# Moving SBUF tiles to other starts modulo 128 bytes in a kernel of 32-bit matmuls on one NeuronCore

## Chip, cores and metric

One core of a Trainium2 chip runs one launch of the kernel. The metric is the device time of the launch in microseconds (us). The kernel before was timed three times: 2841.1 us is the median, 2837.99 and 2863.9 us are the ends.

## What is computed

256 tokens of width 2048 go through two transformer-like blocks. Nearly all the arithmetic is in matrix products of the tokens with float32 weight matrices, about 480 MB of weights in all:

```
# first block
proj   = rms_norm(x) @ w_in                       # 2048 x 11280
y_a    = gated_delta_rule(...) @ w_branch_a       # 8 heads, chunks of 64
y_b    = block_attention(...)  @ w_branch_b       # 8 heads
x      = x + (sigmoid(gate_a) * y_a + sigmoid(gate_b) * y_b) @ w_out
u      = causal_conv(rms_norm(x) @ w_up)          # 2048 x 11264
x      = x + (silu(u_gate) * u_val) @ w_down      # 5632 x 2048
x      = rms_norm(x)
# second block
z      = rms_norm(x) @ w_in_2                     # pooling branch and rwkv7 scan
x      = x + concat(pool_out, rwkv_out) @ w_out_2
x      = x + square(relu(rms_norm(x) @ w_ffn_up)) @ w_ffn_down   # 2048 x 8192 x 2048
x      = x + sigmoid(rms_norm(x) @ w_ple_gate) * (p @ w_ple_proj)
out    = rms_norm(x)
```

## The kernel before

Every large product is made from two float32r parts of each operand, a rounded value (hi) and what is left (lo): hi times hi, hi times lo and lo times hi are added up in PSUM. The weights come in pieces of 512 KB. `load_w` issues the DMA of a piece on SyncE's queue into `raw`, ScalarE copies it to `hi` (line 319) and VectorE subtracts to get `lo` (line 320); each of the three has three buffers. The activations' parts are made once for each product and stay in SBUF: `xhl` holds both parts of the normalized tokens, `hid`, `mh`, `ml`, `oah`, `obh` and others hold those of later stages.

Two helpers issue nearly all matmuls of TensorE.

- `wide_steps` makes outputs with features on the partitions. The weights are the stationary operand, 128 x 128 at a time, and the activations `xhl` stream past: 512 columns for the hi part of the weights (both parts of x, line 373) and 256 columns for their lo part (line 375). These two make a pair.
- `group_steps` makes outputs with tokens on the partitions. The activations are the stationary operand and the weights stream past, 512 columns at a time (256 in two short groups near the end): x hi with weights hi (line 345), x lo with weights hi (346), x hi with weights lo (347).

Each matmul instruction has its own load of the stationary operand (LDWEIGHTS, engine PEld in the profile), which runs beside the matmul ahead of it. In the stages with many small steps (the delta rule from about 200 to 500 us, the rwkv scan from about 1500 to 2000 us) a written-out order puts a few of these matmuls between the steps of a chain of other work.

Pools stack their tiles one behind the other along each partition, each tile at the next multiple of 32 bytes. The first constant table has 129 float32 columns (516 bytes), the small tiles (`tiny`, `rcol`, `hp` and so on) have 8 to 108 bytes, and all large tiles are multiples of 1024 bytes. So a few odd sizes decide where the large tiles start. In the built program they start at these places modulo 128 bytes:

| tile | before |
|---|---|
| `xhl` | 32 |
| `hi`, `lo` (all buffers) | 32 |
| `hid` of the second block; `oah`, `oal`, `mh`, most `ml` | 96 |
| `hid` of the first block: 8 of 11 groups, `obh`, `obl` | 0 |
| `hid` of the first block: 3 of 11 groups | 96 |
| `dhl0`; `dhl1` (pooling) | 96; 32 |

The pieces that one matmul reads of them lie at multiples of 512 bytes from there, except in the two narrow column groups (16 and 32 weight columns).

Of the kernel before, what the change touches and what calls it, by code (L numbers as in the profile page):

```python
# [10 lines left out]
F32 = mybir.dt.float32  # L11
# [8 lines left out]
KT = 16  # L20
KC = 2
NEG = -1e30
WINDOWS = (2, 4, 8, 16)


def _const_tables():
# [5 lines left out]
    def add(tables, name, a):  # L32
        for t in tables:
            t.append((name, np.broadcast_to(a, (128, a.shape[1])).astype(np.float32)))
# [4 lines left out]
    add([t1], "upper", (p <= f))  # L39
    add([t1], "gbias", np.where(p <= f, 0.0, NEG))  # L40
    add([t1], "amask", np.where(f <= p, 0.0, NEG))
    p64, f64 = p % 64, f[:, :64]
# [9 lines left out]
    add([t2], "rst", (np.arange(T)[None, :] % 64 != 0))  # L52
    for w in WINDOWS:
        add([t2], f"pc{w}", 1.0 / np.minimum(np.arange(16)[None, :] + 1, w))
# [67 lines left out]
def two_blocks_kernel(ctx: ExitStack, tc: tile.TileContext, I: dict, out: bass.AP):  # L122
    nc = tc.nc
# [3 lines left out]
    whi = ctx.enter_context(tc.tile_pool(name="whi", bufs=3))  # L127
    wlo = ctx.enter_context(tc.tile_pool(name="wlo", bufs=3))
    tmp = ctx.enter_context(tc.tile_pool(name="tmp", bufs=2))
# [11 lines left out]

    def load_consts(i, pool, queue):
        a, cols = CONSTS[i]
        t = pool.tile([128, a.shape[1]], F32, tag=f"C{i}", name=f"C{i}", bufs=1)
        queue.dma_start(t, I[f"consts{i}"])
        for name, (o, w) in cols.items():
            tabs[name] = t[:, o:o + w]

# [3 lines left out]
    def c(name, lo=0, hi=128):  # L152
        return tabs[name][lo:hi]

    load_consts(0, cpool, nc.sync)
    ident, one = c("ident"), c("one")

# [2 lines left out]
        return PT[t][lo:hi, o + i:o + i + n]  # L160

    cnt = [0]

    def nm(s):
        cnt[0] += 1
        return f"{s}_{cnt[0]}"
# [6 lines left out]
        return quad.tile(list(shape), dt, tag=f"Q{i}", name=nm(name))  # L173

    def tm(tag, F, dt=F32, bufs=2, p=128, pool=None):
        shape = [p] + (list(F) if isinstance(F, (tuple, list)) else [F])
        return (pool or tmp).tile(shape, dt, tag=tag, name=nm(tag), bufs=bufs)

    def wk(tag, F, dt=F32, bufs=2, p=128):
        return tm(tag, F, dt, bufs, p, quad)  # L180

    def psum(F=512, p=128):
        shape = [p] + (list(F) if isinstance(F, (tuple, list)) else [F])
        return ps.tile(shape, F32, tag="ps", name=nm("ps"))
# [26 lines left out]
    def other_params():  # L211
# [7 lines left out]
        for t in range(2):  # L219
            for i in range(NPT[t]):  # L220
                place_params(t, i, min(128, NROW[t] - 128 * i))

    ln_rows = tm("cva", T, bufs=3)[:16, :128]
    nc.scalar.dma_start(ln_rows, I["ln1"].rearrange("o (a b) -> (o a) b", b=128))

# [6 lines left out]
    def rsqrt(dst, src, t):  # L232

        ts(out=t.bitcast(I32), in0=src.bitcast(I32), scalar1=1, scalar2=None, op0=ALU.logical_shift_right)
        ts(out=dst.bitcast(I32), in0=t.bitcast(I32), scalar1=-1, scalar2=0x5F3759DF, op0=ALU.mult, op1=ALU.add)
        for f in (3.0, 12.0, 768.0):
            tt(out=t, in0=dst, in1=dst, op=ALU.mult)
            tt(out=t, in0=t, in1=src, op=ALU.mult)
            stt(dst, t, -f, dst, ALU.add, ALU.mult)
        ts(out=dst, in0=dst, scalar1=-1.0 / 8192, scalar2=None, op0=ALU.mult)  # L240

    def tiny(shape):
        return tm("tiny", shape, bufs=8)
# [145 lines left out]
    def wide(*a, **kw):  # L389
        for _ in wide_steps(*a, **kw):  # L390
            pass
# [117 lines left out]
    def gdn_gates():  # L509
        ab = tm("cva", T, bufs=3)[:16]  # L510
        wide(w_in, 3072, 16, xs, None, lambda m, p: act(ab, p, AF.Copy))
        hp = tm("hp", (2, 8), bufs=1)
        nc.gpsimd.dma_start(hp[:, 0], I["gdn_a_log"][0:1, :].to_broadcast([128, 8]))
        nc.gpsimd.dma_start(hp[:, 1], I["gdn_dt_bias"][0:1, :].to_broadcast([128, 8]))
        abt = tm("abt", (2, 16), bufs=1)
        p = psum()
        for i in range(2):
            nc.tensor.transpose(p[:, i * 16:(i + 1) * 16], ab[:, i * 128:(i + 1) * 128], ident[:16, :16])
        for i in range(2):
            ts(out=abt[:, i], in0=p[:, i * 16:(i + 1) * 16], scalar1=r1[:, i:i + 1], scalar2=None, op0=ALU.mult)  # L520

        act(t0, abt[:, :, 0:8], AF.Exp, scale=-1.0)
        ts(out=t0, in0=t0, scalar1=1.0, scalar2=None, op0=ALU.add)
        nc.vector.reciprocal(beta, t0)

        y = tm("y8", (2, 8), bufs=1)
        tt(out=y, in0=abt[:, :, 8:16], in1=hp[:, 1:2].to_broadcast([128, 2, 8]), op=ALU.add)
        ts(out=t0, in0=y, scalar1=0.0, scalar2=None, op0=ALU.max)
        stt(t1, t0, -2.0, y, ALU.mult, ALU.add)
        act(t1, t1, AF.Exp)  # L530
        sa = tm("sa8", (2, 8), bufs=1)
        s2 = tm("s28", (2, 8), bufs=1)
        ts(out=s2, in0=t1, scalar1=2.0, scalar2=None, op0=ALU.add)
        nc.vector.reciprocal(s2, s2)
        tt(out=sa, in0=t1, in1=s2, op=ALU.mult)
        tt(out=s2, in0=sa, in1=sa, op=ALU.mult)
        ts(out=t1, in0=s2, scalar1=2.0 / 17, scalar2=2.0 / 15, op0=ALU.mult, op1=ALU.add)
        for d in (13, 11, 9, 7, 5, 3, 1):
            tt(out=t1, in0=t1, in1=s2, op=ALU.mult)
            ts(out=t1, in0=t1, scalar1=2.0 / d, scalar2=None, op0=ALU.add)  # L540
        tt(out=t1, in0=t1, in1=sa, op=ALU.mult)
        tt(out=t0, in0=t0, in1=t1, op=ALU.add)
        ea = tm("ea8", 8, bufs=1)
        act(ea, hp[:, 0], AF.Exp)
        for i in range(2):
            stt(g[:, i], t0[:, i], -1.0, ea, ALU.mult, ALU.mult)
        p = psum()
        mm(p[:, 0:16], c("upper"), g, start=True, stop=True)
        mm(p[:, 16:32], c("ones"), g, start=False, stop=True, skip_group_check=True)
        nc.vector.tensor_copy(gc, p[:, 0:16].rearrange("p (a b) -> p a b", a=2))  # L550
        act(eg, gc, AF.Exp)
        tt(out=kds, in0=p[:, 16:32].rearrange("p (a b) -> p a b", a=2), in1=gc, op=ALU.subtract)
        act(kds, kds, AF.Exp)
        stt(nbe, beta, -1.0, eg, ALU.mult, ALU.mult)

    def gdn_scales(half):

        p = psum()
        for m in range(4):
            sq = wk("E", (2, 2, 128), bufs=1)  # L560
            act(sq, kq[half][m // 2][:, m % 2], AF.Square)
            for i in range(2):
                for j in range(2):
                    o = 8 * j + 4 * i + m
                    mm(p[:, o:o + 1], sq[:, i, j], one, start=(m == i == j == 0), stop=True, skip_group_check=True)
        hs = slice(4 * half, 4 * half + 4)
        n = tiny((2, 2, 4))
        ts(out=n, in0=p[:, :16].rearrange("p (a b c) -> p a b c", a=2, b=2), scalar1=1e-6, scalar2=None, op0=ALU.add)
        F = tm("gsc", (6, 2, 4))
        rsqrt(F[:, 0:2], n, tiny((2, 2, 4)))  # L570
        rk, rq, bk, kdr, nber, egq = (F[:, i] for i in range(6))
        ts(out=rq, in0=rq, scalar1=128 ** -0.5, scalar2=None, op0=ALU.mult)
        tt(out=bk, in0=beta[:, :, hs], in1=rk, op=ALU.mult)
        tt(out=kdr, in0=kds[:, :, hs], in1=rk, op=ALU.mult)
        tt(out=nber, in0=nbe[:, :, hs], in1=rk, op=ALU.mult)
        tt(out=egq, in0=eg[:, :, hs], in1=rq, op=ALU.mult)
        return rk, rq, bk, kdr, nber, egq
# [89 lines left out]
    def gdn_half(half):  # L667
        sc = gdn_scales(half)
        yield 12
        pre = []  # L670
        for m in range(4):
            pre.append(gdn_pre(4 * half + m, sc))
            yield 5
        Z = inverse16([p[0][:, 0] for p in pre], 2)
        yield 55
        for _ in rounds(gdn_inverse(pre[m:m + 2], Z[:, m:m + 2]) for m in (0, 2)):
            yield 6
        for m in (0, 2):
            for _ in rounds(gdn_post(4 * half + m + i, sc, pre[m + i]) for i in range(2)):
                yield 5  # L680
# [154 lines left out]
    for _ in gdn_proj(0):  # L835
        pass
    load_consts(1, quad, nc.sync)
    gdn_gates()
    other_params()

# [6 lines left out]
    for j, shift in ((0, 0.25), (1, 0.0)):  # L847

        n = tm("cva", T, bufs=3)[:32]
# [162 lines left out]
    oka = tm("oka", 8, bufs=1)  # L1012
# [16 lines left out]

    wide(w_in2, 4096, 288, xs, lambda: r4, ev_lora)  # L1030
    load_consts(2, quad, nc.sync)
    LW, GW, GV = ([wk(t, (4, 128), bufs=4).rearrange("p a b -> p (a b)") for _ in range(2)] for t in ("L0", "L0", "L1"))
    for q in range(2):
# [7 lines left out]
    for i in range(8):  # L1041
        q, o = divmod(i, 4)
        cols = slice(128 * o, 128 * o + 128)
        p, p2 = psum(), psum()
# [4 lines left out]
        p = psum()  # L1049
# [226 lines left out]
    def pool_proj(q):  # L1276
# [3 lines left out]
        def ev(m, p):  # L1280
            g, o = divmod(m, 2)
            win = WINDOWS[2 * q + g]
            u = tm("junk", T + 16, bufs=1)
# [163 lines left out]
```

## Time and profile before

| | |
|---|---|
| median of three runs | 2841.1 us |
| the profiled execution | 2840.32 us |
| its span, first to last instruction | 2838.5 us |
| TensorE clock granted, mean | 0.985 |
| TensorE busy | 98% of the span |
| VectorE, ScalarE, GpSimd busy | 65%, 49%, 6% |
| DMA | 172 GB/s mean |

A matmul's row in the profile has a start and a duration, and the durations overlap: a 512-column matmul has a duration near 395 ns, but the next one starts some 230 ns after it. The cost of a matmul in a dense stretch is therefore read from the distance between starts, not from the duration. Rows of the timeline give starts to 0.01 us, so the distance is taken over many instructions.

### The profile page before, as it was taken

To read this page: it belongs to the slowest core of one execution; us is meant where nothing else is said; L and a number is where in the kernel's file an instruction comes from. 1 tells how busy PE (TensorE), PEld (TensorE's weight loads), DVE (VectorE), ACT (ScalarE), POOL (GpSimd) and SP (SyncE) were. 2 spreads that over 40 slices of the span, in tenths; PEclk is the share of its full clock that TensorE was granted. 3 is DMA by queue.
4 is the path that set the end of the run, shared out by engine and by line. 5 is a ranking of instruction groups with operands and counts; after the bars stand their busy time and mean duration, and the time that the engine had idled before them with its cause. 6 is when DMAs were issued, how large, how long until landed. Compare 5 with 4: busy or idle time off the path is not lost.

```text
span 2838.5 us, 40515 instructions
## 1 busy us (share of the span) xinstructions
PE 2773.4 (98%) x15538; PEld 2330.5 (82%) x15538; DVE 1856.4 (65%) x2908; ACT 1397.2 (49%) x2088; POOL 159.2 (6%) x217
## 2 busy tenths in 40 slices
PE   9999989999999999999999999899999999999997
PEld 7888877888888888888887777777888888888886
DVE  7786766555577755775666696876765655646555
ACT  6664535444455544554455644334543443434454
POOL 0003300000000000000001120220000000000001
PEclk9999999999999999999999999899999999999999
DMA  7565644666566656665656363253566666666554
GB/s 218 167 178 146 175 135 119 183 187 186 184 187 188 191 189 188 187 186 190 204 185 177 103 161 103 82 140 108 176 192 192 189 191 191 186 192 202 186 185 149
DMA packets 398200, 487.94 MB, mean 172 GB/s; under 512 B 38426, under 2 KB 283173, under 8 KB 398005
## 3 DMA queue, kind: packets, MB, share of 16 engines
q1 hardware_dynamic: 397221, 482.93, 56.5%
q8 instruction: 122, 2.00, 0.3%
q10 hardware_dynamic: 608, 2.11, 0.2%
q14 instruction: 73, 0.60, 0.1%
q0 software_dynamic: 176, 0.30, 0.1%
HBM read 479.25 MB, written 6.03 MB: 171 GB/s over the span
## 4 chain that ended last, share of the span: by engine, by line
PE 91%; DVE 5%; DMA 1%; ACT 1%; issue 1%; POOL 1%; SPq 0%; ACTq 0%; POOLq 0%; DVEq 0%
PE pp L373 28%; PE pp L375 15%; PE pp L345 14%; PE pp L346 14%; PE pp L347 14%; DVE lo L320 1%; PE ps L261 1%; DMA Z<-s 1%; PE ps L736 0%; DVE L L1143 0%; PE ps L1209 0%; PE ps L729 0%; PE ps L1211 0%; POOL X L720 0%; DMA s<-Ei 0%
## 5 line engine op out<-in xcount | busy, mean ns | idle before, releaser
L320 DVE TENSOR_TENSOR lo<-raw,hi 128x1024 fp32r<-128x1024 f32 x902 | 1109.1, 1230 | 809.5 <-ACT hi L319 789.5
L319 ACT ACTIVATE hi<-raw 128x1024 fp32r<-128x1024 f32 x902 | 953.4, 1057 | 1200.6 <-PE pp L346 563.8
L373 PE MATMUL pp<-xhl,hi 128*128 128x512 f32 x3648 | 1292.9, 398 | 2.0 <-DVE z L382 2.0
L375 PE MATMUL pp<-xhl,lo 128*128 128x256 f32 x3648 | 1031.7, 283 | 1.9 <-DVE lo L320 1.9
L373 PEld LDWEIGHTS pp<-xhl,hi 128*128 128x128 f32 x3648 | 684.9, 188 | 164.8 <-DVE z L382 2.4
L375 PEld LDWEIGHTS pp<-xhl,lo 128*128 128x128 f32 x3648 | 689.7, 189 | 9.9 <-issue 4.7
L345 PE MATMUL pp<-hi,hid 128*128 128x512 f32 x864 | 340.0, 394 | 0.0
L347 PE MATMUL pp<-lo,hid 128*128 128x512 f32 x864 | 339.4, 393 | 0.0
L346 PE MATMUL pp<-hi,hid 128*128 128x512 f32 x864 | 338.8, 392 | 0.0
L347 PE MATMUL pp<-lo,xhl 128*128 128x512 f32 (+1 forms) x544 | 206.4, 379 | 0.0
L346 PE MATMUL pp<-hi,xhl 128*128 128x512 f32 (+1 forms) x544 | 206.2, 379 | 0.0
L345 PE MATMUL pp<-hi,xhl 128*128 128x512 f32 (+1 forms) x544 | 205.9, 378 | 0.0
L347 PEld LDWEIGHTS pp<-lo,hid 128*128 128x128 f32 x864 | 162.2, 188 | 37.0
L345 PEld LDWEIGHTS pp<-hi,hid 128*128 128x128 f32 x864 | 162.2, 188 | 36.1
L346 PEld LDWEIGHTS pp<-hi,hid 128*128 128x128 f32 x864 | 162.2, 188 | 36.0
L345 PEld LDWEIGHTS pp<-hi,xhl 128*128 128x128 f32 x544 | 102.4, 188 | 18.6
L346 PEld LDWEIGHTS pp<-hi,xhl 128*128 128x128 f32 x544 | 102.4, 188 | 18.4
L347 PEld LDWEIGHTS pp<-lo,xhl 128*128 128x128 f32 x544 | 102.4, 188 | 18.2
L927 DVE TENSOR_TENSOR x<-x,pp 128x512 f32<-128x512 f32 x96 | 61.6, 683 | 32.5 <-PE pp L347 32.5
L382 DVE TENSOR_TENSOR z<-pp,z 128x512 f32<-128x512 f32 (+2 forms) x119 | 80.8, 679 | 1.3 <-ACT z L381 1.1
L384 DVE TENSOR_TENSOR z<-z,rstd 128x512 f32<-128x512 f32 x114 | 78.3, 688 | 3.3
L281 POOL TENSOR_TENSOR junk<-x,rows 128x512 f32<-128x512 f32 x8 | 13.4, 1676 | 1114.7 <-ACT junk L278 1114.7
(415 smaller groups left out, 2539.4 us busy)
## 6 DMA issues: line engine op xcount, KB each, us to landing
raw<-in_w_in_dram SPq DMA_DIRECT2D x244, 512.0 KB, 3.7
raw<-in_w_up_dram SPq DMA_DIRECT2D x176, 512.0 KB, 3.6
raw<-in_w_ffn_up_dram SPq DMA_DIRECT2D x128, 512.0 KB, 3.7
raw<-in_w_ffn_down_dram SPq DMA_DIRECT2D x128, 512.0 KB, 3.7
raw<-in_w_down_dram SPq DMA_DIRECT2D x88, 512.0 KB, 4.3
raw<-in_w_out_dram SPq DMA_DIRECT2D x64, 512.0 KB, 3.8
raw<-in_w_ple_gate_dram SPq DMA_DIRECT2D x32, 512.0 KB, 4.0
raw<-in_w_branch_a_dram SPq DMA_DIRECT2D x16, 512.0 KB, 4.2
```

What stands on the lines that cost most here:

```text
L261: nc.tensor.transpose(p[:w, m - m0, i * 128:(i + 1) * 128], src[:, i, 128 * m:128 * m + w], ident)
L281: nc.gpsimd.tensor_tensor(out=y, in0=s, in1=self.w2[j], op=ALU.mult)
L319: act(h, r, AF.Copy)
L320: tt(out=l, in0=r, in1=h.bitcast(F32), op=ALU.subtract)
L345: mm(p, xh, h[:, j], start=(k == 0), stop=False, skip_group_check=True)
L346: mm(p, xl, h[:, j], start=False, stop=False, skip_group_check=True)
L347: mm(p, xh, l[:, j], start=False, stop=last, skip_group_check=True)
L373: mm(P[:w, m].rearrange("p a b -> p (a b)"), h[:, j, f], x2.rearrange("p a b -> p (a b)"), start=(k == 0), stop=False, skip_group_check=True)
L375: mm(P[:w, m, 0], l[:, j, f], x2[:, 0], start=False, stop=last, skip_group_check=True)
L382: tt(out=z, in0=P[:w, :nw, 0], in1=z, op=ALU.add)
L384: tt(out=z, in0=z, in1=r()[:w].unsqueeze(1).to_broadcast([w, nw, T]), op=ALU.mult)
L927: tt(out=s, in0=s, in1=p, op=ALU.add)
```

## The change

Tile sizes in the pools are rounded up, mostly to whole 128-byte lines (`LINE` is 32 float32 columns), with five kinds of small tiles rounded to 64 or 32 bytes. The first constant table is rounded up too. A 64-byte tile, `step0`, is put at the start of the pool of `hi`, and one, `step1`, at the start of `tmp`; each is set to zero once on GpSimd. Some small tiles of the first block move from `tmp` to the phase's pool. No shape of an operand and no computation changes.

```diff
+LINE = 32
 ...
     def load_consts(i, pool, queue):
         a, cols = CONSTS[i]
-        t = pool.tile([128, a.shape[1]], F32, tag=f"C{i}", name=f"C{i}", bufs=1)
-        queue.dma_start(t, I[f"consts{i}"])
+        t = pool.tile([128, -(-a.shape[1] // LINE) * LINE], F32, tag=f"C{i}", name=f"C{i}", bufs=1)
+        queue.dma_start(t[:, :a.shape[1]], I[f"consts{i}"])
 ...
     cnt = [0]
+    for i, pool in enumerate((whi, tmp)):
+        nc.gpsimd.memset(pool.tile([128, LINE // 2], F32, tag="step", name=f"step{i}", bufs=1), 0.0)
 ...
     def tm(tag, F, dt=F32, bufs=2, p=128, pool=None):
-        shape = [p] + (list(F) if isinstance(F, (tuple, list)) else [F])
-        return (pool or tmp).tile(shape, dt, tag=tag, name=nm(tag), bufs=bufs)
+
+        shape = list(F) if isinstance(F, (tuple, list)) else [F]
+        n = math.prod(shape)
+        line = {"tiny": LINE // 2, "rcol": LINE // 2, "PC": LINE // 4, "nacc": LINE // 2, "oka": LINE // 2}.get(tag, LINE)
+        t = (pool or tmp).tile([p, -(-n // line) * line], dt, tag=tag, name=nm(tag), bufs=bufs)[:, :n]
+        names = " ".join(f"a{i}" for i in range(len(shape)))
+        return t.rearrange(f"p ({names}) -> p {names}", **{f"a{i}": d for i, d in enumerate(shape)})
 ...
-        hp = tm("hp", (2, 8), bufs=1)
+        hp = wk("hp", (2, 8), bufs=1)
 ...                                  # the same for abt, y8, sa8, s28, ea8 and gsc
```

In the built program of the changed kernel `xhl`, `hid`, `mh`, `ml`, `oah`, `obh`, `dhl` and all other activation tiles start at 0 modulo 128, and all buffers of `hi` and `lo` at 64. So in `wide_steps` the streaming operand starts at 0 and the stationary one at 64, and in `group_steps` it is the other way round. On TensorE, VectorE, ScalarE and SyncE the same instructions stand in the same order as before; GpSimd has the two memsets more, at its start.

## Rows read from the trace of the kernel before

**Rows 1.** Page, busy time and share of each engine.
```profile
PE 2773.4 (98%) x15538; PEld 2330.5 (82%) x15538; DVE 1856.4 (65%) x2908; ACT 1397.2 (49%) x2088; POOL 159.2 (6%) x217
```
**Rows 2.** Page, the chain that ended last, by engine and by line.
```profile
PE 91%; DVE 5%; DMA 1%; ACT 1%; issue 1%; POOL 1%; SPq 0%; ACTq 0%; POOLq 0%; DVEq 0%
PE pp L373 28%; PE pp L375 15%; PE pp L345 14%; PE pp L346 14%; PE pp L347 14%; DVE lo L320 1%; PE ps L261 1%; DMA Z<-s 1%; PE ps L736 0%; DVE L L1143 0%; PE ps L1209 0%; PE ps L729 0%; PE ps L1211 0%; POOL X L720 0%; DMA s<-Ei 0%
```
**Rows 3.** Groups by line: shapes, count, busy us, mean ns, idle before and releaser.
```profile
L373 PE MATMUL pp<-xhl,hi 128*128 128x512 f32 x3648 | 1292.9, 398 | 2.0 <-DVE z L382 2.0
L320 DVE TENSOR_TENSOR lo<-raw,hi 128x1024 fp32r<-128x1024 f32 x902 | 1109.1, 1230 | 809.5 <-ACT hi L319 789.5 <-PE ps L261 14.0 <-PE pp L375 3.6
...
L345 PE MATMUL pp<-hi,hid 128*128 128x512 f32 x864 | 340.0, 394 | 0.0
...
L345 PE MATMUL pp<-hi,xhl 128*128 128x512 f32 (+1 forms) x544 | 205.9, 378 | 0.0
```
**Rows 4.** Timeline of PE (start us, us, line): `group_steps`, stationary `xhl`, first and last.
```profile
2755.68 0.39 PE L347 MATMUL pp<-lo,xhl 128*128 128x512 f32 x1
...
2775.85 0.39 PE L346 MATMUL pp<-hi,xhl 128*128 128x512 f32 x1
```
**Rows 5.** Timeline of PE: `group_steps`, stationary `hid` at 96, first and last.
```profile
2149.78 0.39 PE L345 MATMUL pp<-hi,hid 128*128 128x512 f32 x1
...
2169.93 0.39 PE L346 MATMUL pp<-hi,hid 128*128 128x512 f32 x1
```
**Rows 6.** Timeline of PE: `group_steps`, stationary `hid` at 0, first and last.
```profile
1049.64 0.39 PE L345 MATMUL pp<-hi,hid 128*128 128x512 f32 x1
...
1069.94 0.40 PE L345 MATMUL pp<-hi,hid 128*128 128x512 f32 x1
```
**Rows 7.** Timeline of PE: `group_steps` with 256 columns, first and last.
```profile
2804.73 0.28 PE L347 MATMUL pp<-lo,xhl 128*128 128x256 f32 x1
...
2814.93 0.28 PE L345 MATMUL pp<-hi,xhl 128*128 128x256 f32 x1
```
**Rows 8.** Timeline of PE: `wide_steps` near 900 us, first and last.
```profile
899.80 0.39 PE L373 MATMUL pp<-xhl,hi 128*128 128x512 f32 x1
...
919.90 0.39 PE L373 MATMUL pp<-xhl,hi 128*128 128x512 f32 x1
```
**Rows 9.** Timeline of PE: `wide_steps` near 1200 us, first and last.
```profile
1199.73 0.40 PE L373 MATMUL pp<-xhl,hi 128*128 128x512 f32 x1
...
1220.93 0.40 PE L373 MATMUL pp<-xhl,hi 128*128 128x512 f32 x1
```
**Rows 10.** Timeline of PE: `wide_steps` with a stationary operand of 16 columns, first and last.
```profile
82.06 0.39 PE L373 MATMUL pp<-xhl,hi 128*16 128x512 f32 x1
...
87.27 0.39 PE L373 MATMUL pp<-xhl,hi 128*16 128x512 f32 x1
```
**Rows 11.** Timeline of PE at 1815 us, streaming `dhl1`.
```profile
1815.07 0.63 PE L373 MATMUL pp<-dhl,hi 128*128 128x512 f32 x1
1815.50 0.41 PE L375 MATMUL pp<-dhl,lo 128*128 128x256 f32 x1
1815.71 0.63 PE L373 MATMUL pp<-dhl,hi 128*128 128x512 f32 x1
```
**Rows 12.** Windows: us; busy us (count) of PE, PEld, DVE, ACT, POOL; PEclk, DMA share, GB/s.
```profile
1814.90:1816.30 1.40, 1.40 (x6) 1.21 (x5) 1.37 (x2) 0.00 (x0) 0.00 (x0) 0.50 0.87 307
900.00:920.00 20.00, 20.00 (x117) 17.64 (x116) 14.64 (x20) 11.31 (x17) 0.00 (x0) 1.00 0.63 192
200.00:500.00 300.00, 287.71 (x1812) 244.71 (x1811) 201.93 (x456) 145.48 (x269) 52.93 (x56) 0.97 0.52 146
1500.00:2000.00 500.00, 469.98 (x3388) 377.04 (x3386) 364.95 (x703) 231.88 (x462) 84.87 (x138) 0.95 0.44 125
```
**Rows 13.** Timeline of PE: `wide_steps` streaming `dhl0`, which starts at 96.
```profile
1803.31 0.40 PE L373 MATMUL pp<-dhl,hi 128*128 128x512 f32 x1
...
1804.01 0.40 PE L373 MATMUL pp<-dhl,hi 128*128 128x512 f32 x1
```

More of the change, by code (lines that the diff above doesn't have):

```diff
@@ L511, in gdn_gates @@
         wide(w_in, 3072, 16, xs, None, lambda m, p: act(ab, p, AF.Copy))
-        hp = tm("hp", (2, 8), bufs=1)
+        hp = wk("hp", (2, 8), bufs=1)
         nc.gpsimd.dma_start(hp[:, 0], I["gdn_a_log"][0:1, :].to_broadcast([128, 8]))
         nc.gpsimd.dma_start(hp[:, 1], I["gdn_dt_bias"][0:1, :].to_broadcast([128, 8]))
-        abt = tm("abt", (2, 16), bufs=1)
+        abt = wk("abt", (2, 16), bufs=1)
         p = psum()
@@ L524, in gdn_gates @@
         nc.vector.reciprocal(beta, t0)
-        y = tm("y8", (2, 8), bufs=1)
+        y = wk("y8", (2, 8), bufs=1)
         tt(out=y, in0=abt[:, :, 8:16], in1=hp[:, 1:2].to_broadcast([128, 2, 8]), op=ALU.add)
@@ L530, in gdn_gates @@
         act(t1, t1, AF.Exp)
-        sa = tm("sa8", (2, 8), bufs=1)
-        s2 = tm("s28", (2, 8), bufs=1)
+        sa = wk("sa8", (2, 8), bufs=1)
+        s2 = wk("s28", (2, 8), bufs=1)
         ts(out=s2, in0=t1, scalar1=2.0, scalar2=None, op0=ALU.add)
@@ L542, in gdn_gates @@
         tt(out=t0, in0=t0, in1=t1, op=ALU.add)
-        ea = tm("ea8", 8, bufs=1)
+        ea = wk("ea8", 8, bufs=1)
         act(ea, hp[:, 0], AF.Exp)
@@ L568, in gdn_scales @@
         ts(out=n, in0=p[:, :16].rearrange("p (a b c) -> p a b c", a=2, b=2), scalar1=1e-6, scalar2=None, op0=ALU.add)
-        F = tm("gsc", (6, 2, 4))
+        F = wk("gsc", (6, 2, 4))
         rsqrt(F[:, 0:2], n, tiny((2, 2, 4)))
```

## The prediction

> **What bounds the kernel now.** I read the page's busy times first: TensorE is busy 98% of the span, no other engine over 65% [rows 1]. The chain that ended last agrees: 91% of it is TensorE, and nearly all of that lies on the five matmul lines of the two helpers [rows 2]. The groups by line show no waiting ahead of these matmuls, 2.0 us or less in a group of hundreds, while VectorE's `lo`, the next largest, waits 789.5 us for ScalarE [rows 3]. The windows show that the two stages with a chain of small steps are the only long stretches where TensorE stands idle: 300 - 287.7 = 12.3 us in the delta rule and 500 - 470.0 = 30.0 us in the scan [rows 12]. So the time is a count of matmuls times the distance between their starts, and a change of the distance goes nearly whole into the total.
>
> That distance comes from first and last starts. In `group_steps`: with the stationary operand at 32 modulo 128, 89 steps in 20.17 us, 226.6 ns [rows 4]; at 96, 88 steps in 20.15 us, 229.0 ns [rows 5]; at 0, 87 steps in 20.30 us, 233.3 ns [rows 6]. In all three the streaming weights start at 32, the shapes are equal and the clock is full. With 256 columns, 85 steps in 10.20 us, 120.0 ns [rows 7]. In `wide_steps` a pair (512 and 256 columns) takes 20.10 / 58 = 346.6 ns in one stretch [rows 8] and 21.20 / 60 = 353.3 ns in another [rows 9], with the same residues; the timeline changes from one to the other and back, and each holds about half of the stretches, so 350 is the mean.
>
> What would they be with nothing lost? One stretch ran at a granted clock of 0.50 [rows 12], that is at 1.2 instead of 2.4 GHz, and there 512 columns take 0.43 us and 256 take 0.21 us [rows 11], which is columns divided by the clock. At full clock that makes 213.3 and 106.7 ns. The best dense rows lie 13.3 ns above it with 512 columns (226.6) and 13.3 ns above it with 256 (120.0), and the best pair 346.6 - 320.0 = 26.6 = 2 x 13.3. So each matmul carries a constant of 13.3 ns, whatever its length. It isn't the weight load's length: with 16 stationary columns instead of 128 the pair is still 5.21 / 15 = 347.3 ns [rows 10]. And it shows only where the columns run at 2.4 GHz.
>
> 13.3 ns is the time of 32 float32 columns, 128 bytes, at 2.4 GHz. An operand that streams from 32 modulo 128 touches 17 lines of 128 bytes where 16 would do, and 9 instead of 8 with 256 columns: one line more for each matmul, exactly the constant. That is an interpretation, since every float32r operand that streams in this trace starts at 32 or 96 modulo 128, and no row has one at 0 or 64. What the rows do show is that a start modulo 128 matters: 226.6, 229.0 and 233.3 differ in nothing else of the matmul.
>
> **The change part by part.** *Order and waits.* The four engines that matter keep their instructions in their order, so no wait is added. The two memsets of 64 bytes stand on GpSimd, which is busy 6% [rows 1]; they end before the first weights have landed, and without that cover they would cost well under the 1 us that can't be told here. The moved small tiles change nobody's buffers. These cost nothing.
>
> *`wide_steps`, 3,648 pairs [rows 3]*, of which about 3,550 run dense at full clock (the rest stand beside the chains or at half clock). The streaming `xhl` moves from 32 to 0, the stationary weights from 32 to 64. The lower end is 320 ns, nothing lost. The upper end is 360: the worse of the two rhythms, 353.3, and 6.7 more, the step by which rows 6 lie above rows 4. I take 333.3, half of the 26.6 removed. If the unit is the 128-byte line, all of it could go; if the unit is half a line, a start at 32 costs half of it and the other half is something else, and the different places of the two operands, 64 apart, may eat a part: at that distance the trace has one `group_steps` row at 2.4 over the best [rows 5], and a pair near 353 where `dhl0` at 96 streams [rows 13]. Gain: 3,550 x (350 - 333.3) = 59 us.
>
> *`group_steps`.* The count is 3 x (864 + 544) for the two large groups [rows 3] and 3 x 400 for the other operands, 5,424; 192 of these have 256 columns, and 5,090 of the others run dense. By the tiles' places about 1,470 have the stationary operand at 32 (226.6 ns), 2,600 at 96 (229.0) and 1,020 at 0 (233.3): a mean of 229.2. As a check, 3,550 x 0.350 + 5,090 x 0.2292 + 192 x 0.120 = 2,432 us, and the remaining 408 us of the execution are the small products of the chains, the waits around them and the start and end. Now the streaming weights go to 64 and the stationary activations to 0. Ends: 213.3 (nothing lost) and 240 (233.3 and one step of 6.7 more). I take 220.0, again half of the constant; at 64 modulo 128 a whole-line rule alone would give nothing here, a half-line rule half of it. Gain: 5,090 x 9.2 = 47 us, and 192 x 6.7 ns = 1 us.
>
> *What is late next.* In the dense stretches DMA has a share of 0.63 and VectorE 14.6 of 20 us [rows 12]; 5% more demand leaves both under 0.8, so they stay hidden. In the delta rule and the scan the chain of small steps is hidden by these same matmuls, and shorter matmuls hide less of it. Windows of 800 us lie there [rows 12]; at the share of dense matmuls that I count in them (some 830 pairs and 1,035 of `group_steps`) they hold 23 us of the gain, and I let half of it, 12 us, come back as waiting.
>
> Sum: 59 + 47 + 1 - 12 = 95 us off the profiled execution's 2840.3 us, 2745 us. That execution lies 0.8 us under the median of 2841.1, so nothing is added. A change within 1%, 28 us, can't be told from none by a measurement of this kernel.
>
> [...]
>
> **The rivals.** *A. Nothing to tell.* The 13.3 ns are a fixed price of a float32r matmul at full clock, and only the distance between the two operands' starts matters. Then it is 64 everywhere: `group_steps` goes to the 229.0 of rows 5 (1,470 x +2.4 and 1,020 x -4.3, -1 us), and pairs settle at 346.6 (-12 us) or 353.3 (+12 us): 2828 to 2852, about 2840. For it: the constant is equal in every row, and nothing here streams from 0 or 64. Against it: at half clock the constant is gone, which a fixed price in either clock would not do.
>
> *B. Slower.* The stationary operand's own place decides. The slowest distance of the trace is that with the stationary operand at 0 [rows 6], and the change puts it there in all of `group_steps`: 5,090 x (233.3 - 229.2) = +21 us. If the pairs too hold the slower rhythm throughout, 3,550 x 3.3 ns = +12 us: 2873 us. It is over 1% once the pairs go beyond about 352 while `group_steps` stands at 233. Against it: in rows 6 the stationary operand at 0 met a stream at 32, and this pairing doesn't occur any more.
>
> *C. One helper alone.* Whole lines count, so streaming from 0 gives `wide_steps` nearly all its 26.6 ns (3,550 x 25 = 89 us), while `group_steps`, streaming from 64, stays at 229: 2840 - 89 + 10 given back = 2761 us. With half-lines alone and a loss by the 64 bytes' distance, 2790.
>
> *D. More than forecast*, both helpers near the columns' own time, 323 and 216 ns: 96 + 67 less 18 given back, 2695 us.
>
> **How the numbers follow.** Forecast and C, which I count as one family with its centre at 2745 to 2790: 0.52. D: 0.08. A: 0.25. B: 0.15. The predicted time is 2745 us. For the range I leave out the lower part of D and B: from 2712, a little over D, to 2855, the upper end of A. Faster by over 1% is the forecast, C and D: 0.60. Within 1%: A, 0.24. Slower by over 1%: B and the worst of A, 0.16. The family's own range is 2712 to 2800 us.
>
> **What will show it.** In the trace after: distances between starts near 333 ns for a pair of lines 373 and 375 (now eight lines lower in the file) and near 220 ns in `group_steps`, alike in all stages where before there were three values, because every stationary operand now starts at the same place. If whole lines count, the pair falls below 330 and the 512-column distance in `group_steps` stays over 226, with 120 ns at 256 columns. If A holds, 229 and 346 to 353. If B, 233 and more. TensorE's idle time in the scan and the delta rule should grow from 42 us by some 12. The prediction fails if the constant of 13.3 ns stays where the stream starts at 0, which only a run can show, or if two operands 64 bytes apart disturb each other more than rows 5 lets see.

## The result and the profile after

The changed kernel takes 2860.5 us at the median of 20 runs (2850.6 to 2872.9), the kernel before 2841.8 us at the median of 20 (2838.0 to 2863.9); the ratio is 1.0067, 95% interval 1.0052 to 1.0082. The change is inside 1%, but the interval leaves no doubt that it is slower, where 2745 us was forecast; the prediction's remark that a change within 1% can't be told from none doesn't hold for 20 runs of each kernel.

One thing is needed to read the single times: runs with a mean clock under 0.983 take some 10 to 20 us more (one run of `all0` below, 3896.2 us at 0.651, is left out of that kernel's ratio), and in each of the five of them that were profiled (`all0`, `all32`, `all256`, `best96` and `best224`, mean clock 0.977 to 0.980) TensorE ran at half clock for a stretch of 41 to 44 us, which begins between 1559 and 1573 us; in the four 10-us windows of `best96` from 1560 to 1600 us the granted clock is 0.51, 0.50, 0.50 and 0.50. Of the 20 times of the changed kernel 9 have such a low clock (median 2871.0 us), the 11 others have a median of 2855.8 us. The profiled executions compared here, 2855.83 us after and 2840.32 us before, both have a mean clock of 0.985, and neither has that stretch (1.00 from 1560 to 1600 us in both). So 15.5 us are to be explained from the two traces.

The page of the changed kernel: busy time of each engine, then the chain that ended last.

```profile
PE 2786.6 (98%) x15538; PEld 2332.6 (82%) x15538; DVE 1858.4 (65%) x2908; ACT 1398.0 (49%) x2088; POOL 158.0 (6%) x219
...
PE 91%; DVE 4%; DMA 1%; ACT 1%; POOL 1%; issue 1%; SPq 0%; ACTq 0%; POOLq 0%; DVEq 0%
PE pp L381 28%; PE pp L383 14%; PE pp L355 14%; PE pp L354 14%; PE pp L353 14%; DVE lo L328 1%; PE ps L269 1%; DMA Z<-s 0%; POOL pool L1298 0%; PE ps L744 0%; DMA s<-Ei 0%; PE ps L1217 0%; DVE L L1151 0%; PE ps L1219 0%; POOL X L728 0%
```

The bound hasn't moved: TensorE is busy 98% and holds 91% of the chain, as in [rows 1, 2]; lines lie eight lower. Its busy time grew by 2786.6 - 2773.4 = 13.2 us. The groups by line say in which matmuls (busy us, mean ns, idle before):

```profile
L381 PE MATMUL pp<-xhl,hi 128*128 128x512 f32 x3648 | 1304.9, 400 | 1.9 <-DVE z L390 1.9
...
L353 PE MATMUL pp<-hi,hid 128*128 128x512 f32 x864 | 338.2, 391 | 0.0
...
L353 PE MATMUL pp<-hi,xhl 128*128 128x512 f32 (+1 forms) x544 | 207.0, 380 | 0.0
```

Against [rows 3] the wide matmul has 12.0 us more, and of the line that multiplies the hi parts in `group_steps` the groups with `hid` have 1.8 less and those with `xhl` 1.1 more, with the same counts and no waiting. The distances from one start to the next show it better. Timeline of TensorE in the changed kernel (start us, us, line), first and last of six stretches, and three rows at half clock:

```profile
899.79 0.40 PE L381 MATMUL pp<-xhl,hi 128*128 128x512 f32 x1
...
919.93 0.40 PE L381 MATMUL pp<-xhl,hi 128*128 128x512 f32 x1
...
1048.80 0.39 PE L354 MATMUL pp<-hi,hid 128*128 128x512 f32 x1
...
1069.80 0.39 PE L354 MATMUL pp<-hi,hid 128*128 128x512 f32 x1
...
1199.61 0.40 PE L381 MATMUL pp<-xhl,hi 128*128 128x512 f32 x1
...
1220.81 0.40 PE L381 MATMUL pp<-xhl,hi 128*128 128x512 f32 x1
...
1826.71 0.63 PE L381 MATMUL pp<-dhl,hi 128*128 128x512 f32 x1
1827.14 0.41 PE L383 MATMUL pp<-dhl,lo 128*128 128x256 f32 x1
1827.35 0.63 PE L381 MATMUL pp<-dhl,hi 128*128 128x512 f32 x1
...
2149.68 0.39 PE L353 MATMUL pp<-hi,hid 128*128 128x512 f32 x1
...
2169.82 0.39 PE L354 MATMUL pp<-hi,hid 128*128 128x512 f32 x1
...
2771.65 0.39 PE L354 MATMUL pp<-hi,xhl 128*128 128x512 f32 x1
...
2791.79 0.39 PE L355 MATMUL pp<-lo,xhl 128*128 128x512 f32 x1
...
2814.80 0.28 PE L354 MATMUL pp<-hi,xhl 128*128 128x256 f32 x1
...
2831.99 0.28 PE L353 MATMUL pp<-hi,xhl 128*128 128x256 f32 x1
```

A pair near 900 us is now 20.14 / 57 = 353.3 ns where it was 346.6 [rows 8]; near 1200 us it stays 21.20 / 60 = 353.3 [rows 9]. In `group_steps` `xhl` goes from 226.6 [rows 4] to 20.14 / 88 = 228.9 ns; `hid` of the second block stays at 20.14 / 88 = 228.9 [rows 5] and `hid` of the first block at 21.00 / 90 = 233.3 [rows 6], though their starts modulo 128 are now equal. 256 columns take 17.19 / 146 = 117.7 ns, 2.3 less than [rows 7]. At half clock 512 and 256 columns still take 0.43 and 0.21 us, as in [rows 11]. The windows (busy us and counts of PE, PEld, DVE, ACT, POOL; clock, DMA share, GB/s):

```profile
900.00:920.00 20.00, 20.00 (x115) 17.38 (x114) 14.53 (x21) 11.40 (x16) 0.00 (x0) 1.00 0.60 188
...
200.00:500.00 300.00, 287.65 (x1809) 243.72 (x1808) 203.91 (x457) 145.64 (x267) 51.09 (x56) 0.97 0.52 147
1500.00:2000.00 500.00, 468.64 (x3378) 375.16 (x3377) 361.71 (x699) 230.53 (x459) 88.26 (x140) 0.95 0.44 124
```

The idle time in the two stages of small steps is 12.4 and 31.4 us, 1.4 more than in [rows 12]; the waits are not where the time went.

The means over the whole traces close the account. They are distances from one start to the next, over all pairs and all 512-column matmuls of `group_steps` in dense stretches at full clock. Pairs: 349.8 before, 353.1 after, 3,478 x 3.3 = +11.5 us. `group_steps`: 229.5 before, 230.1 after, 5,090 x 0.65 = +3.3 us. Together +14.8 of the 15.5 us.

### The profile page after: what moved, and what is told of

It reads as the page before. It is cut to its first block, busy times and chain, and to the rows that moved or that the text cites. A ratio compares the mean times of both kernels' runs of the same rounds, so it can differ in the third digit from the quotient of the medians.

```text
span 2854.1 us, 40522 instructions
## 1 busy us (share of the span) xinstructions
PE 2786.6 (98%) x15538; PEld 2332.6 (82%) x15538; DVE 1858.4 (65%) x2908; ACT 1398.0 (49%) x2088; POOL 158.0 (6%) x219
## 4 chain that ended last, share of the span: by engine, by line
PE 91%; DVE 4%; DMA 1%; ACT 1%; POOL 1%; issue 1%; SPq 0%; ACTq 0%; POOLq 0%; DVEq 0%
PE pp L381 28%; PE pp L383 14%; PE pp L355 14%; PE pp L354 14%; PE pp L353 14%; DVE lo L328 1%; PE ps L269 1%; DMA Z<-s 0%; POOL pool L1298 0%; PE ps L744 0%; DMA s<-Ei 0%; PE ps L1217 0%; DVE L L1151 0%; PE ps L1219 0%; POOL X L728 0%
```

## The experiments

Below, *distance* means the start of the stationary operand minus the start of the streaming one, modulo 256 bytes. The starts are those of the built programs. In the kernel before nearly all pairs have distance 0, `group_steps` has 0 with `xhl`, 192 with `hid` of the second block, 224 with most of the first block's. In the changed kernel the pairs have 64, `group_steps` has 192, and 64 with most of the first block's `hid`, since those lie in slots at 128 modulo 256. Three theories stood against each other. That of the prediction (L in the expectations): where the stream starts decides, and 0 modulo 128 removes the constant of 13.3 ns. The prediction's rival B (O in the first expectations): the stationary operand's own place decides. The distance theory (D in the expectations, not the prediction's rival D): only the distance between the two starts counts, first taken modulo 128, then, as D256, modulo 256.

**1. Matmuls by themselves, 16 pairings of starts** (`probe1`). All blocks of the model are left out. What is left are rows of 96 equal matmuls, then rows of 48 pairs, with the streaming operand at 0, 32, 64, 96 modulo 128 and the stationary one too, and the same in bfloat16 (`bm`, `bs`) and with fewer columns:

```diff
+    for am in (0, 32, 64, 96):
+        for st in (0, 32, 64, 96):
+            group(M[am], S[st])
 ...                                  # the same for pairs
+    for n in (128, 256, 384):
+        group(M[0], S[0], n)
 ...
+    for n in (128, 256, 512):
+        group(bm, bs, n)
```

> This kernel leaves the blocks out and copies x to its output. With no other engine at work, TensorE runs blocks of 96 matmuls for every pairing of four starts of the streaming and four of the stationary operand (0, 32, 64, 96 modulo 128), in the form of group_steps (512 columns) and of wide_steps (pairs of 512 and 256), then blocks of 128, 256 and 384 columns at starts 0/0 and 32/32 and of bf16. Theory D (only the distance of the two starts counts): the four pairings at distance 0 are alike and fastest, 226.7 ns and a pair of 346.7 or 353.3; 64 apart 229 and 353; the pairing 32 streaming, 0 stationary 233. Theory L (whole lines of the streaming operand, as in the prediction): pairings that stream from 0 fall to 213 to 220 and 320 to 333. Theory O (the stationary operand's own place): all pairings with the stationary operand at 0 are the slowest, 233. [...]

The timeline of this kernel folds equal matmuls that stand in a row: start, us from the first start to the last end, and their count. `ma` streams from 0; `sa` and `sc` are stationary, 64 bytes apart modulo 128.

```profile
60.75 20.62 PE L49 MATMUL pp<-ma,sa 128*128 128x512 f32 x88
...
105.69 19.62 PE L49 MATMUL pp<-ma,sc 128*128 128x512 f32 x85
...
686.80 9.43 PE L49 MATMUL pp<-ma,sa 128*128 128x128 f32 x83
...
697.25 10.01 PE L49 MATMUL pp<-ma,sa 128*128 128x256 f32 x83
...
769.76 8.46 PE L49 MATMUL pp<-bm,bs 128*128 128x256 bf16 x76
```

Less the last one's own duration, this is (20.62 - 0.40) / 87 = 232.4 ns with both starts at 0 modulo 128, and 228.9 with the stationary operand 64 further. The four pairings with equal starts, at 0, 32, 64 and 96, have 232.3 to 232.4: the place itself does nothing. With 256 columns it is 118.7 ns, and in bfloat16 (8.46 - 0.27) / 75 = 109.2; 512 columns in bfloat16 have a mean of 215.8. The columns' own time is an estimate: 768 columns take 0.64 us at a granted clock of 0.50 [rows 11, 12], 1.2 a ns, which doubled to full clock makes 213.3 ns for 512; 256 columns more cost 215.8 - 109.2 = 106.6 ns here in bfloat16, and 226.6 - 120.0 = 106.6 in float32r [rows 4, 7], 2.4 a ns. The price above that time stays where the stream starts at 0, and in bfloat16 it is 2.5 ns. It isn't one constant for every length either: at these equal starts it is 19.1 ns with 512 columns, 16.0 with 384 (a mean of 176.0), 12.0 with 256, and with 128 columns, (9.43 - 0.27) / 82 = 111.7, it is 58. Whether it is the data type as such or the four bytes of each column instead of two wasn't tried. The equal pairings should have given the 226.6 of [rows 4] if the distance modulo 128 were all; in this kernel such operands lay 128 apart modulo 256, and that made the next question.

**2. The same modulo 256** (`probe2`; again the blocks are left out). 16 stationary tiles, each 8 float32, 32 bytes, further, with the access pattern of the two helpers, against a stream at 128 (`W`) and one at 160 (`V`) modulo 256:

```diff
+    for j in range(16):
+        group(W, S[j], 8 * j)
+    for j in range(16):
+        wide(W, S[j], 8 * j)
+    for j in range(16):
+        group(V, S[j], 8 * j)
+    for j in range(16):
+        wide(V, S[j], 8 * j)
 ...                                  # steps of 4 bytes, repeats at 0, fewer stationary columns
```

> This kernel leaves the blocks out and copies x to its output. Blocks of 96 matmuls in the order of group_steps and 64 pairs in the order of wide_steps, no other engine at work, at 16 distances of the stationary operand's start from the streaming one's, 0 to 480 bytes in steps of 32, first with the stream at 128 and then with it at 160 modulo 256. Then distances of 4 to 32 bytes in steps of 4, repeats of the pair at distance 0 behind short blocks of different length, and pairs with 64, 32 and 16 stationary columns. Theory D256 (only the distance modulo 256 counts): both halves of the scan alike, 0 and 256 alike; group_steps at 226.7 for 0, 229.0 for 192, 233.3 for 64 and 224, 232.4 for 128; pairs at 346.7 or 353.3 for 0, 353.3 for 64, 346.7 for 96 and 224. Theory A (absolute starts count): the two halves differ at equal distance by 2 ns and more. Theory P (the period is 128): 0 and 128 alike, 64 and 192 alike, 96 and 224 alike. The pair at distance 0 behind different blocks: one rhythm throughout if the operands alone decide, two if the moment of the start does.

Timeline, pairs: first and last 512-column matmul of the tile at distance 0 and of that at 96, 63 pairs each.

```profile
376.84 0.39 PE L69 MATMUL pp<-wa,sa 128*128 128x512 f32 x1
...
399.09 0.40 PE L69 MATMUL pp<-wa,sa 128*128 128x512 f32 x1
...
444.65 0.40 PE L69 MATMUL pp<-wa,sd 128*128 128x512 f32 x1
...
466.50 0.39 PE L69 MATMUL pp<-wa,sd 128*128 128x512 f32 x1
```

353.2 ns at distance 0, 346.8 at 96. Means of all tiles, in ns:

| distance modulo 256 | 0 | 32 | 64 | 96 | 128 | 160 | 192 | 224 |
|---|---|---|---|---|---|---|---|---|
| `group_steps`, 512 columns | 226.7 | 233.3 | 233.3 | 234.3 | 232.4 | 233.3 | 228.9 | 233.3 |
| `wide_steps`, a pair | 346.6 or 353.3 | 353.5 | 353.3 | 346.7 | 351.1 | 350.0 | 353.3 | 346.7 |

The same eight values come back 256 bytes further and with the other stream. At distance 0 the pair takes either of two rhythms: set again behind six short blocks of other lengths, the same tile settled three times at 346.7 and three times at 353.3 ns. The three values of [rows 4 to 6] are the entries at 0, 192 and 224. One row in `probe1` departs from the table. Of its two rows of 48 pairs at distance 192 one has 353.2 ns, and this is the other, first and last pair:

```profile
534.57 0.39 PE L57 MATMUL pp<-mb,sd 128*128 128x512 f32 x1
...
550.96 0.40 PE L57 MATMUL pp<-mb,sd 128*128 128x512 f32 x1
```

16.39 / 47 = 348.7 ns; so a second rhythm may not be a matter of distance 0 alone, and for pairs the distance modulo 256 doesn't settle everything.

The last rows of this kernel have fewer stationary columns, at distance 0. With 64 of them, first and last of 48 pairs:

```profile
1939.01 0.39 PE L69 MATMUL pp<-wa,sa 128*64 128x512 f32 x1
...
1955.00 0.39 PE L69 MATMUL pp<-wa,sa 128*64 128x512 f32 x1
```

15.99 / 47 = 340.2 ns, less than any pair with 128 columns; with 32 and 16 columns the means are 348.3 and 349.7. So the number of stationary columns does bear on the price; the prediction had ruled that out by a row with 16 of them [rows 10].

**3. All large operands at 0, and all at 32, modulo 128** (`all0`, `all32`). The two step tiles are taken out; the last line, which puts 32 bytes ahead of everything, is in the second kernel alone:

```diff
-    for i, pool in enumerate((whi, tmp)):
-        nc.gpsimd.memset(pool.tile([128, LINE // 2], F32, tag="step", name=f"step{i}", bufs=1), 0.0)
+    nc.gpsimd.memset(cpool.tile([128, LINE // 4], F32, tag="step", name="step", bufs=1), 0.0)
```

> The changed kernel without its two 64-byte tiles: activations and both parts of the weights start at 0 modulo 128. Theory D (distance): group_steps at 226.7 everywhere, pairs at 346.7 or 353.3 by stretch; about 2815 to 2828 us, faster than before by 0.5 to 1%. Theory L (whole lines): under 2780 us. Theory O (stationary operand at 0 is slow): group_steps at 233, pairs at 353 or more, 2860 to 2880 us.

> The same, with one tile of 32 bytes ahead of all others: every activation and both parts of the weights start at 32 modulo 128, as xhl, hi and lo did before, but hid and the other activations too. Theory D: the same as with all at 0, 2815 to 2828 us. Theory L: 2815 to 2830, and slower than with all at 0 by 40 us and more. Theory O: group_steps at 226.7, pairs as before, 2828 us, and faster than with all at 0 by 30 us and more.

`all0`: 2844.2 us, ratio 1.0012 (0.9997 to 1.0027). `all32`: 2849.4 us, 1.0029 (1.0010 to 1.0048). The timeline, `group_steps` with `hid` of the second block, first and last of 88, of `all0` and then of `all32`:

```profile
2149.66 0.39 PE L351 MATMUL pp<-hi,hid 128*128 128x512 f32 x1
...
2169.87 0.40 PE L351 MATMUL pp<-hi,hid 128*128 128x512 f32 x1
```
```profile
2149.63 0.40 PE L353 MATMUL pp<-hi,hid 128*128 128x512 f32 x1
...
2169.86 0.39 PE L353 MATMUL pp<-hi,hid 128*128 128x512 f32 x1
```

232.3 and 232.5 ns, the value of distance 128, which these operands have in both kernels. The pairs are at distance 0 and have the same mean, 349.7. Starts at 0 are worth no more than starts at 32: the prediction's theory and B fall. Half of the 5.2 us between the two medians is the clock (at 0.983 and more they are 2844.0 and 2846.5 us); the other half isn't explained. The 2815 to 2828 us that the distance theory expected didn't come either, because it counted modulo 128, and these `hid` operands stand at 128.

**4. The distance set on purpose** (`all256`, `w64`, `w96`). `all256` brings every large operand but `dhl1` to 0 modulo 256; `w64` and `w96` then set the weights' parts 64 or 96 further. With that the `xhl` operand of `group_steps` gets 192 or 160, all others keep 0, since their pool is moved along. The diff is that of `w96`; `w64` has 16 for 24, and `all256` sets the second of the two tiles alone:

```diff
-        t = pool.tile([128, -(-a.shape[1] // LINE) * LINE], F32, tag=f"C{i}", name=f"C{i}", bufs=1)
+        n = -(-a.shape[1] // LINE) * LINE + (LINE if i == 1 else 0)
+        t = pool.tile([128, n], F32, tag=f"C{i}", name=f"C{i}", bufs=1)
 ...
-        nc.gpsimd.memset(pool.tile([128, LINE // 2], F32, tag="step", name=f"step{i}", bufs=1), 0.0)
+        nc.gpsimd.memset(pool.tile([128, (24, LINE)[i]], F32, tag="step", name=f"step{i}", bufs=1), 0.0)
```

> The changed kernel without the 64-byte tile ahead of the weights, with 128 bytes ahead of the small tiles and 128 more in the second constant table: all operands of the large products start at 0 modulo 256 (dhl1 alone at 128). Theory D256: group_steps at 227 in every stage, pairs as before at 346.7 or 353.3, about 350; 2831 us, ratio 0.996. Theory P: the same as with all at 0 modulo 128, 2844 us, ratio 1.001. Theory L (lines): under 2780 us.

> From the kernel with all at 0 modulo 256: the weights and every activation but xhl start 64 bytes later. The pairs stand at a distance of 64, as in the changed kernel, group_steps over xhl at 192, all other group_steps stay at 0. Theory D256: pairs at 353.1 in every stage (+12 us), group_steps over xhl at 229 (+2.5 us): 14 us more than the kernel with all at 0 modulo 256, 2845 us. Theory A: the same as that kernel, 2831 us.

> The same with 96 bytes: pairs at a distance of 96, group_steps over xhl at 160. Theory D256: pairs at 346.7 in every stage (-11 us against 350), group_steps over xhl at 233.3 (+8 us): 2828 us, the least of all. Theory A: 2831 us. Theory P: pairs as slow as at 224 would be alike, and group_steps over xhl at the value of 32, nothing to tell from D256 here.

| kernel | pairs: distance, ns | `group_steps` with `xhl`, ns | with the others, ns | median us | ratio (95%) |
|---|---|---|---|---|---|
| `all256` | 0, 352.2 | 227.3 | 227 | 2848.4 | 1.0015 (0.9996 to 1.0034) |
| `w64` | 64, 353.2 | 229.1 | 227 | 2844.5 | 1.0015 (1.0000 to 1.0029) |
| `w96` | 96, 346.9 | 233.4 | 227 | 2831.3 | 0.9963 (0.9951 to 0.9975) |

Each distance comes out as the microbenchmark gave it. `w64` also takes the change apart: its pairs are those of the changed kernel, and its `group_steps` differs from it only in operands that have 0 instead of 192 or 64; the profiled span is 2843.0 us against 2854.1, where the means of `group_steps`, 227.6 and 230.1 ns, would make 5,090 x 2.5 ns = 12.7 us. The time of `all256` came out wrong, 17 us over the 2831 expected: in the profiled run its pairs took the slow rhythm more often (352.2 against 349.7 in `all0`), and 7 of its 12 runs have the low clock that goes with the stretch of half clock; the five others have a median of 2835.0.

**5. One number alone** (`best0`, `best64`, `best96`, `best224`). `w96` beat the kernel before, but all its runs had a clock of 0.984 to 0.986, and two distances were changed at once. Here, on the layout of `all256`, the tiles of the weights' parts are 64 columns longer and the wide helper alone writes and reads them from a shifted place, so that `group_steps` keeps distance 0 with every operand. Four kernels differ in that shift only. The room comes from `junk`, which shares the buffers of `z`. The diff is that of `best96`, a shift of 24 columns, 96 bytes; the others have 0, 16 (64 bytes) and 56 (224), and the tile of `lo` is changed like that of `hi`:

```diff
-    def load_w(W, k0, nk, c0, ncol):
+    def load_w(W, k0, nk, c0, ncol, o=0):
-        h = whi.tile([128, nk, ncol], F32R, tag="hi", name=nm("hi"))
+        h = whi.tile([128, nk * ncol + 64], F32R, tag="hi", name=nm("hi"))[:, o:o + nk * ncol].rearrange("p (t c) -> p t c", c=ncol)
...
-                h, l = load_w(W, kc, n, c0 + o0, n2)
+                h, l = load_w(W, kc, n, c0 + o0, n2, 24)
```

> Control of four kernels that differ in one number alone, the place of the weights' parts in the wide helper; the stationary operand of the token helper starts at the same place modulo 256 as its stream in all four. Here the wide helper has distance 0 too. Theory (the distance modulo 256 decides): pairs in two rhythms, a mean of 349.7 to 352.2 ns as in the kernels with distance 0 so far; the token helper 227 ns; 2833 to 2841 us, or some 15 us more where the long stretch of half clock near 1550 us comes. Rival (the faster time of the kernel at 96 came from the clock, which was .984 to .986 in all its runs): all four kernels alike, each scattering between 2825 and 2855 with the clock.

> The wide helper's weights at 64 modulo 256, as far from the stream as in the changed kernel, and nothing else. Theory: pairs 353.1 ns, the token helper 227; 3,470 x (353.1 - 346.9) = 21.5 us over the kernel with 96, 2845 us. Rival: as the control.

> The wide helper's weights at 96 modulo 256, nothing else. Theory: pairs 346.9 ns; the token helper at 227 with the x operand too, which was at 233.4 in the kernel at 96 before: 2831.3 - 1,373 x 6.1 ns = 2823 us. Rival: as the control.

> The wide helper's weights at 224 modulo 256, which is 96 modulo 128, nothing else. Theory: pairs 346.7 ns by the microbenchmark, 2823 us, like the kernel with 96. Rival: as the control.

| kernel | pair, mean ns | median us, all runs | runs at a clock of 0.983 or more: count, median us | ratio (95%) |
|---|---|---|---|---|
| `best0` | 351.8 | 2838.7 | 7 of 12, 2836.1 | 0.9993 (0.9971 to 1.0016) |
| `best64` | 353.1 | 2840.6 | 11 of 12, 2840.5 | 1.0001 (0.9989 to 1.0013) |
| `best96` | 346.8 | 2828.8 | 6 of 12, 2821.0 | 0.9953 (0.9937 to 0.9970) |
| `best224` | 346.8 | 2830.4 | 4 of 8, 2820.7 | 0.9952 (0.9936 to 0.9968) |

The timeline of the pairs near 900 us in `best0`, `best64` and `best96`, first and last of 57, 57 and 58 pairs:

```profile
899.81 0.40 PE L381 MATMUL pp<-xhl,hi 128*128 128x512 f32 x1
...
919.95 0.40 PE L381 MATMUL pp<-xhl,hi 128*128 128x512 f32 x1
```
```profile
899.78 0.28 PE L383 MATMUL pp<-xhl,lo 128*128 128x256 f32 x1
...
919.92 0.28 PE L383 MATMUL pp<-xhl,lo 128*128 128x256 f32 x1
```
```profile
899.81 0.28 PE L383 MATMUL pp<-xhl,lo 128*128 128x256 f32 x1
...
919.92 0.28 PE L383 MATMUL pp<-xhl,lo 128*128 128x256 f32 x1
...
2756.62 0.39 PE L355 MATMUL pp<-lo,xhl 128*128 128x512 f32 x1
...
2776.79 0.39 PE L354 MATMUL pp<-hi,xhl 128*128 128x512 f32 x1
```

20.14 / 57 = 353.3, 353.3 and 20.11 / 58 = 346.7 ns. `best0` has here the slow rhythm, where the kernel before, at the same distance 0, has the fast one [rows 8]. In `best96` the `xhl` operand of `group_steps` takes 20.17 / 89 = 226.6 ns, where `w96` had 233.4. At a clock of 0.983 or more 96 is 19.4 us under 64 (21.5 expected), and 224 equals 96. The rival, that the gain of `w96` was the clock, falls: a low clock comes in `best96` as often as in `best0`, in 6 and 5 of 12 runs, and the kernel is 15 us faster all the same. The expected 2823 us hold for runs without it; the medians of all runs are 6 to 7 us higher.

Windows of the stretch that changes the clock (columns as above), of `best0` and then of `best96`, both profiled runs:

```profile
1555.00:1610.00 55.00, 53.34 (x249) 36.37 (x248) 27.67 (x47) 37.07 (x63) 1.87 (x4) 1.00 0.37 102
```
```profile
1555.00:1610.00 55.00, 53.42 (x145) 32.40 (x145) 15.74 (x29) 22.33 (x39) 0.19 (x1) 0.58 0.20 58
```

In the scan's first steps 249 matmuls run in 55 us at full clock, and 145 in the same time at a mean of 0.58. TensorE is idle 1.7 and 1.6 us in them. Ahead of it, where the first small steps of the scan leave it without work, the 10-us windows sum to 3.4 us idle from 1530 to 1570 us in `best0`, whose clock then stays full, and to 3.8 us from 1520 to 1560 us in `best96`, whose clock then falls to 0.50. These two traces don't tell why.

## Why the prediction was wrong

*What bounds the kernel* was right: TensorE by the count of its matmuls times the time from one start to the next, before and after, and no wait took the change up.

*The constant of 13.3 ns for each float32r matmul at full clock* was measured rightly and read wrongly. This is the step that failed: "one line more for each matmul, exactly the constant". The coincidence with the time of 32 columns carried the whole forecast, though no row had a stream at 0. A run could show it, and the prediction had named this as the sign of its being wrong: the price is there at every start that was tried (226.7 = 213.3 + 13.4 at best). Nor is it "a constant of 13.3 ns, whatever its length" (12.0 to 19.1 ns with 256 to 512 columns in `probe1`, 58 with 128), and "It isn't the weight load's length" was read from 16 stationary columns alone, where 64 give 340.2 ns for a pair. In bfloat16, where 512 and 256 columns take 215.8 and 109.2 ns, only 2.5 ns of it are left. For float32r no row of 512 columns with 128 stationary ones came under 226. So the terms of 59 and 47 us had no source. The prediction's 1.2 and 2.4 GHz stand for columns a ns at a granted clock of 0.50 and 1.00; the rows show those rates and no frequency.

*The starts modulo 128* hid the variable. The argument "226.6, 229.0 and 233.3 differ in nothing else" was right, but what differs is the distance to the stream modulo 256, 0, 192 and 224. The three numbers fit a table by the stationary operand's own place, by the distance modulo 128 or by that modulo 256; `all0` against `all32` excludes the first, and `probe1` against [rows 4] the second.

*`wide_steps`*: -59 us forecast, +11.5 measured. The two rhythms were seen [rows 8, 9] and treated as a mean; they belong to distance 0, and at 64 the pairs have the slow value throughout. The "pair near 353" of [rows 13] is 0.70 us for two pairs, too short to tell 350 from 353. *`group_steps`*: -47 forecast, +3.3 measured, 2.3 us of it from `xhl`, which went from distance 0 to 192 (1,375 x 1.7 ns). Most of the first block's `hid` went from 224 to 64, 233.3 in both. *256 columns*: 192 x 2.3 ns = 0.4 us gained of the 1 forecast. *What is late next*: the 12 us given back had nothing to give back; the idle time grew by 1.4 us. *Order, waits and the two memsets* cost nothing, as said (the memsets take 0.16 us, 0.74 us after the start).

*The rivals.* A named the mechanism, "only the distance between the two operands' starts matters", and its upper end, pairs at 353.3 everywhere, is what happened: 2852 us, against 2855.8 measured without the half-clock stretch. It was off by 4 us in `group_steps`, for which it took 229.0 everywhere, because it knew the distance modulo 128 only. It got a chance of 0.25, because the constant is gone at half clock; that remains true and unexplained, and it didn't bear on the choice. B gave the pairs' +12 us and for `group_steps` +21, of which 3 came. D's 323 and 216 ns are in no run: the least with 128 stationary columns are 346.6 and 226.6. The range ended at 2855, called A's upper end, though A's own sum ends at 2852. The times without the low clock, 2855.8, lie only 0.8 us over it; the median of all lies 5.5 us over it because 9 of the 20 have the low clock, for which the prediction had no term. The kernel before had it in 4 of the 77 runs made beside the experiments.

What stays open: what in the chip makes the distance count, and why a matmul of float32r has 13.3 ns more. Also why the stretch of half clock near 1570 us comes in half of the runs of some layouts, in one of 12 of `best64` and in none of 5 of `w96`. Only one execution of each kernel left a trace; for the others the stretch is inferred from their mean clock.

## What to carry to other kernels

Before a constant is called alignment, look for a row in which the alignment is already what the change would make it; where there is none, a microbenchmark of a few hundred matmuls answers it, and a coincidence of size does not. When places in SBUF seem to matter, tabulate differences between operands as well as places, with more than one modulus. Among steps of 32 bytes float32r matmuls of 512 columns are best here with both starts equal modulo 256 (226.7 ns), and pairs of 512 and 256 columns with 96 or 224 between them (346.7 ns); giving each helper its own shift inside the weights' tile has both, and is 0.5% faster than the kernel before.

## What the runs showed of the hardware that was not expected

- In these runs the time from one float32r matmul's start to the next depends on the stationary operand's start in SBUF minus the stream's, modulo 256 bytes: 226.7 to 234.3 ns with 512 columns, 346.7 to 353.5 ns for a pair, at any absolute start that was tried, but for one row of pairs, 348.7 ns at 192. In the microbenchmarks no other engine is at work beside these rows, and the places of TensorE's own two operands alone make up to 3% (226.7 against 234.3 ns).
- Steps finer than 32 bytes count too, but none helps: over the eight steps of 4 bytes from 4 to 32 in `probe2` rows of 96 matmuls have 230.7 to 235.0 ns (178.8 us / 768 = 232.8 over all), and pairs 346.7 (at 24 bytes) to 353.6 (at 20).
- Pairs at distance 0 have two stable rhythms, 346.7 and 353.3 ns, held for 20 us and more ([rows 8], [rows 9], the repeats in `probe2`); behind six blocks of different lengths each came three times.
- A float32r matmul of 512 columns with 128 stationary ones costs at least 13.3 ns over the 213.3 of its columns at full clock (226.6, [rows 4]); at half clock a pair takes 0.64 us [rows 11], which leaves nothing over its columns to the 0.01 us of a row. A bfloat16 one has 2.5 ns at full clock (215.8).
- Half clock over 41 to 44 us of the scan costs 15 to 19 us (medians of the runs with a low clock and without: 2854.8 and 2836.1 in `best0`, 2836.4 and 2821.0 in `best96`), as much as the layout.
